# Unread products of ones at the norm boundaries, a later square, and feed-forward rounds over two weight tiles

## Chip, core and metric

The kernel runs on one core of one Trainium2 chip. The metric is the device time of one launch in microseconds (us), the median of the runs. The engines of the core are TensorE (PE, matrix products; PEld is its loading of stationary tiles), VectorE (DVE), ScalarE (ACT), GpSimd (POOL) and SyncE (SP, which issues the DMA transfers here).

## What is computed

One layer of an encoder on 256 tokens of width 2048, in float32: a SwiGLU feed-forward block, attention with 16 heads, and a second feed-forward block, each behind an RMS norm that a modulation vector scales and shifts.

```python
mod = jax.nn.silu(c) @ w_ada + b_ada
sh1, sc1, gt1, sh2, sc2, gt2, sh3, sc3, gt3 = jnp.split(mod, 9, axis=-1)
f = swiglu(modulate(rms_norm(h, g_ffn1), sh1, sc1), w1_gate, w1_up, w1_down)
h = h + 0.5 * gt1 * f
qkv = modulate(rms_norm(h, g_mix), sh2, sc2) @ w_qkv
...
h = h + gt2 * (jnp.concatenate([o_na, o_dil], -1) @ w_o)
f = swiglu(modulate(rms_norm(h, g_ffn2), sh3, sc3), w2_gate, w2_up, w2_down)
h = h + 0.5 * gt3 * f
```

## The kernel before

**Layout.** Features lie on the 128 partitions, the 256 tokens on the free axis. `h` is 16 tiles of 128x256. A normed input `nx[k]` (16 tiles) is kept as two halves of 256 columns, a rounded part and the rest, so that a product in the fast float32 format loses little: the rounded weights (`hi`, the cast of L146 on ACT) are multiplied with both halves in one product of 512 columns (L353), the rest of the weights (`lo`, the subtraction of L149 on DVE) with the first half alone, in one of 256 columns (L355). In qkv (L637, L640) the weights are the moving side, and all products have 512 columns.

**The weight stream.** All weights pass through one stream of tiles of 128x1024, eight blocks of 128x128 each. A tile is loaded by SP (L140, five buffers), cast on ACT (L146) and subtracted on DVE (L149); of `hi` and `lo` there are four buffers each (`LOB`). `W.add` collects eight products, takes the next tile with `chunk`, and issues eight products with `hi`, then eight with `lo`: one *round*. `prepare` keeps the stream three tiles ahead (`AHEAD`) and, at a rate given by `pace`, interleaves the 144 products of the modulation vector (*ada*, L129, 2.3 us each on DVE, with 1 MB of weights each).

**Stages.** A startup with six input tiles as the first rounds allow (L514); the first feed-forward's up products (`pa`, `pb`), its down products (`pd`, L417 adds them to `h`) over 32 of the 44 hidden tiles, then up and down over the other 12; qkv as 96 units of one tile with the attention heads woven in; the output projection as 32 units (`wo_unit`, `pso`); the second feed-forward in the same way as the first. The ends of the first feed-forward and of the output projection are the two *norm boundaries* of this text: `Stat` squares each tile of `h` (ACT, L195; the last one on DVE, L193) and adds the squares up on DVE (L185); TensorE sums them over the partitions by a product with ones (L208, L209); `rstd_from` turns that into the norm's factor (L168 to L173); `norm_pair` makes two `nx` tiles (L222 on DVE, L223 on ACT, L225 on DVE). TensorE's next product needs the first pair. The other seven pairs follow while the first eight units or rounds run; unit or round number *i* needs pair *i* (counted from 0).

**What sets the order.** Outside of `manual_schedule` a scheduler orders each engine's instructions at build time; in the range of the boundaries (`BORDER`: PE, DVE, ACT) they stand as the program writes them. Every engine works through its instructions in order.

## Time and profile before

| | |
|---|---|
| time, median of 3 runs | 1939.87 us (1939.45 to 1940.7) |
| time of the profiled execution | 1940.85 us |
| its span, first to last instruction | 1939.0 us |
| PE busy | 1900.1 us (98%) |
| DVE busy | 1524.3 us (79%) |
| ACT busy | 902.8 us (47%) |
| first product of L514 in the startup | 19.40 us |
| end of the first feed-forward, first qkv product | 768.6 us, 775.08 us |
| last product of the output projection, first of the second feed-forward | 1179.1 us, 1195.88 us |

A row of the trace's timeline gives the start and the length of a merged run of equal instructions; products overlap by their tails, so the pace of a run is read from start to start. PEclk is the TensorE clock that was granted, as a share of 2.4 GHz; 0.50 is 1.2 GHz.

### The profile page before, as it was taken

How to read it: one execution, taken by the hardware profiler on the slowest of the kernel's cores; microseconds unless marked ns; L12 is line 12 of the kernel's file. 1: busy time of each engine (PE TensorE's matmuls, PEld its weight loads, DVE VectorE, ACT ScalarE, POOL GpSimd, SP SyncE). 2: the span in 40 equal slices, each digit the busy share in tenths (PEclk: the TensorE clock that was granted, in tenths of full speed). 3: DMA queues.
4: the chain of work that ended last, by engine and by line, in shares of the span. 5: the costliest groups of instructions: out<-in, count | busy, mean ns of one | idle time of the engine just before them, and what ended most of it. 6: DMA issues, size and time to landing. Idle time of an engine off the chain costs nothing.

```text
span 1939.0 us, 27422 instructions
## 1 busy us (share of the span) xinstructions
PE 1900.1 (98%) x10528; PEld 1653.7 (85%) x10528; DVE 1524.3 (79%) x2058; ACT 902.8 (47%) x1327; POOL 0.7 (0%) x6
## 2 busy tenths in 40 slices
PE   8999999999999998999999997999999999999999
PEld 6888888888888887888788886888888888888888
DVE  7999999999788888799977897668865655545665
ACT  2545444433344454555555654544444433334442
POOL 0000000000000000000000000000000000000000
PEclk9999999999999999999999998999999999999999
DMA  9998888889988888589854453669866556656664
GB/s 400 404 362 310 312 309 302 312 330 408 343 308 341 314 312 292 199 329 323 321 192 163 153 157 105 198 213 321 321 206 186 189 189 187 193 187 188 190 194 134
DMA packets 120084, 503.98 MB, mean 260 GB/s; under 512 B 13329, under 2 KB 15633, under 8 KB 101521
## 3 DMA queue, kind: packets, MB, share of 16 engines
q1 hardware_dynamic: 119952, 502.24, 73.8%
q8 instruction: 82, 1.34, 0.3%
q14 instruction: 50, 0.40, 0.1%
HBM read 500.09 MB, written 2.10 MB: 259 GB/s over the span
## 4 chain that ended last, share of the span: by engine, by line
PE 90%; DVE 5%; DMA 2%; issue 1%; ACT 1%; SPq 0%; ACTq 0%; DVEq 0%
PE pb L353 29%; PE pd L353 16%; PE pb L355 15%; PE pd L355 8%; PE pqv L637 3%; PE pqk L637 3%; PE pqq L637 3%; PE pa L353 3%; PE pa L514 2%; DVE low L149 2%; PE pqv L640 2%; DMA ra<-in_w_ada_dram 2%; PE pa L355 1%; PE pqk L640 1%; PE pqq L640 1%
## 5 line engine op out<-in xcount | busy, mean ns | idle before, releaser
L146 ACT CAST hiw<-rw 128x1024 fp32r<-128x1024 f32 x644 | 674.0, 1050 | 784.5 <-PE pd L353 228.8
L149 DVE TENSOR_TENSOR low<-rw,hiw 128x1024 fp32r<-128x1024 f32 x644 | 782.7, 1221 | 302.7 <-ACT hiw L146 300.0
L353 PE MATMUL pb<-nx,hiw 128*128 128x512 f32 x2432 | 610.7, 393 | 4.1 <-DVE nx L225 4.1
L353 PEld LDWEIGHTS pb<-nx,hiw 128*128 128x128 f32 x2432 | 438.5, 189 | 83.3 <-issue 4.8
L355 PEld LDWEIGHTS pb<-nx,low 128*128 128x128 f32 x2432 | 332.3, 191 | 24.8 <-DVE low L149 1.2
L353 PE MATMUL pd<-hd,hiw 128*128 128x512 f32 x1384 | 346.7, 392 | 0.0
L355 PE MATMUL pb<-nx,low 128*128 128x256 f32 x2432 | 339.9, 283 | 0.5 <-DVE low L149 0.5
L353 PEld LDWEIGHTS pd<-hd,hiw 128*128 128x128 f32 x1384 | 248.9, 189 | 44.4
L129 DVE CUSTOM_DVE_ANT_0 ra<-ra,cb,vec 128x2048 f32<-128x2048 f32 x109 | 255.6, 2345 | 15.7 <-DMA ra<-in_w_ada_dram 15.3
L355 PEld LDWEIGHTS pd<-hd,low 128*128 128x128 f32 x1408 | 191.8, 190 | 14.0 <-DVE low L149 0.7
L355 PE MATMUL pd<-hd,low 128*128 128x256 f32 x1408 | 196.4, 282 | 0.3 <-DVE low L149 0.3
L417 DVE SCALAR_TENSOR_TENSOR h<-pd,m,h 128x256 f32<-128x256 f32 x126 | 59.4, 480 | 57.6 <-PE pd L355 57.2
L129 DVE CUSTOM_DVE_ANT_0 rx<-rx,cb,vec 128x2048 f32<-128x2048 f32 x35 | 82.1, 2345 | 3.7 <-DMA rx<-in_w_ada_dram 3.7
L353 PE MATMUL pa<-nx,hiw 128*128 128x512 f32 x288 | 72.3, 393 | 0.0
L637 PE MATMUL pqv<-hiw,nx 128*128 128x512 f32 x256 | 66.1, 401 | 3.5 <-ACT nx L223 3.5
L637 PE MATMUL pqk<-hiw,nx 128*128 128x512 f32 x256 | 65.0, 396 | 0.0
L637 PE MATMUL pqq<-hiw,nx 128*128 128x512 f32 x256 | 64.6, 394 | 0.0
L674 PE MATMUL pso<-ox,hiw 128*128 128x512 f32 x240 | 61.8, 401 | 0.0
L637 PEld LDWEIGHTS pqv<-hiw,nx 128*128 128x128 f32 x256 | 48.9, 194 | 13.9 <-ACT nx L223 3.9
L353 PEld LDWEIGHTS pa<-nx,hiw 128*128 128x128 f32 x288 | 51.9, 189 | 9.3
L637 PEld LDWEIGHTS pqq<-hiw,nx 128*128 128x128 f32 x256 | 46.8, 188 | 9.1
L637 PEld LDWEIGHTS pqk<-hiw,nx 128*128 128x128 f32 x256 | 46.5, 188 | 8.9
(145 smaller groups left out, 1380.9 us busy)
## 6 DMA issues: line engine op xcount, KB each, us to landing
ra<-in_w_ada_dram SPq DMA_DIRECT2D x109, 1024.0 KB, 7.3
rw<-in_w_b_dram SPq DMA_DIRECT2D x200, 512.0 KB, 4.4
rw<-in_w_d_dram SPq DMA_DIRECT2D x128, 512.0 KB, 4.3
rw<-in_w_c_dram SPq DMA_DIRECT2D x96, 512.0 KB, 3.6
rw<-in_w_qkv_dram SPq DMA_DIRECT2D x96, 512.0 KB, 4.7
rx<-in_w_ada_dram SPq DMA_DIRECT2D x35, 1024.0 KB, 7.5
rw<-in_w_e_dram SPq DMA_DIRECT2D x48, 512.0 KB, 4.1
rw<-in_w_a_dram SPq DMA_DIRECT2D x44, 512.0 KB, 6.8
```

What stands on the lines that cost most here:

```text
L129: dot = nc.vector.tensor_tensor_reduce(out=raw, in0=raw, in1=cb, scale=1.0, scalar=vec[:, BA + i : BA + i + 1], op0=ALU.mult, op1=ALU.add, ...
L146: cast = nc.scalar.copy(hi, raw)
L149: nc.vector.tensor_tensor(lo, raw, hi.bitcast(F32), ALU.subtract)
L353: nc.tensor.matmul(out, w, r, start=first, stop=False)
L355: nc.tensor.matmul(out[:, :S], lo[:, b * P : (b + 1) * P], r[:, 0, :], start=False, stop=last)
L417: nc.vector.scalar_tensor_tensor(h[d], part_, gate(d), h[d], ALU.mult, ALU.add)
L514: nc.tensor.matmul(pa[f][:, q, :], w[:, b * P : (b + 1) * P], full[k], start=k == 0 and q == 0, stop=k == K1 - 1 and q == 1, skip_group_ch ...
L637: nc.tensor.matmul(ps[t], nx[k][:, i, t * P : (t + 1) * P], whi[:, kk * 512 : (kk + 1) * 512], start=k + i == 0, stop=False)
L640: nc.tensor.matmul(ps[t], nx[k][:, 0, t * P : (t + 1) * P], wlo[:, kk * 512 : (kk + 1) * 512], start=False, stop=k == KT - 1)
L674: nc.tensor.matmul(ps, w, o, start=kk == 0, stop=False)
```

## The change

`keep_warm(n)` multiplies `ones` with `ones` n times into a bank that nobody reads. It is called with 16 in the startup ahead of L514, and at both norm boundaries with 4 ahead of the two products of the statistic and with 13 behind them.

In the last six units of the output projection the square of a tile of `h` is taken within the next unit, behind that unit's copy on ACT. At both boundaries one weight tile fewer is prepared ahead of the statistic (`ws.ahead`), and it follows behind the first pairs.

`W.add` takes two tiles at a time (`group`) from the first feed-forward's `ffn_rest` on, and in the second feed-forward from its third hidden tile on; the last four output tiles of each feed-forward go by single tiles as before. In the second feed-forward every other group is *turned*: its `lo` products come first if the group before it ended in `lo`, apart from accumulators that are new in it. The host lays out the weights of the up products accordingly (`halves`).

```diff
@@ -46,6 +46,8 @@
 AHEAD = 3
 RAWB = 5
 WARM = 8
+WA = 4
+WB = 13
 ARA = 2
 ARX = 1
 LOB = 4
...
@@ -86,6 +88,12 @@
+
+        def keep_warm(n):
+            ps = bank("warm")
+            for i in range(n):
+                nc.tensor.matmul(ps[:, :P], ones, ones, start=True, stop=True)
...
@@ -305,6 +313,10 @@
                 self.ready = {}
                 self.rate = 0.0
                 self.credit = 0.0
+                self.ahead = AHEAD
+                self.group = 1
+                self.turn = False
+                self.ended_lo = False

             def fetch(self, n):
                 while self.head < n:
@@ -315,7 +327,8 @@
                 self.tail += 1
                 return self.ready.pop(self.tail - 1)

-            def prepare(self, ahead=AHEAD, pin=False):
+            def prepare(self, ahead=None, pin=False):
+                ahead = self.ahead if ahead is None else ahead
                 while self.head <= min(self.tail + ahead, len(srcs) - 1):
                     self.ready[self.head] = wsplit(wraw(srcs[self.head]), pin)
                     self.head += 1
...
-            def chunk(self):
-                self.prepare()
+            def chunk(self, ahead=None):
+                self.prepare(ahead)
                 self.tail += 1
                 return self.ready.pop(self.tail - 1)

-            def add(self, out, r, first, last, then=None, whole=False):
-                self.todo.append((out, r, first, last, whole))
+            def add(self, out, r, first, last, then=None, whole=False, key=None):
+                self.todo.append((out, r, first, last, whole, key))
                 if then:
                     self.thens.append(then)
-                if len(self.todo) < 8:
+                if len(self.todo) < 8 * self.group:
                     return
-                hi, lo = self.chunk()
+                tiles = [self.chunk(self.ahead - i) for i in range(self.group)]
                 todo, thens = self.todo, self.thens
                 self.todo, self.thens = [], []
-                for b, (out, r, first, last, whole) in enumerate(todo):
-                    w = hi[:, b * P : (b + 1) * P]
+                new = {t[5] for t in todo if t[2]}
+                early = [b for b, t in enumerate(todo) if t[5] not in new] if self.turn and self.ended_lo else []
+                late = [b for b in range(len(todo)) if b not in early]
+
+                def weights(b, half):
+                    return tiles[b // 8][half][:, b % 8 * P : (b % 8 + 1) * P]
+
+                def low(b, stop):
+                    out, r = todo[b][:2]
+                    nc.tensor.matmul(out[:, :S], weights(b, 1), r[:, 0, :], start=False, stop=stop)
+
+                for b in early:
+                    low(b, False)
+                for b, (out, r, first, last, whole, key) in enumerate(todo):
+                    w = weights(b, 0)
+                    stop = last and b in early
                     if whole:
                         nc.tensor.matmul(out[:, :S], w, r[:, 0, :], start=first, stop=False)
-                        nc.tensor.matmul(out[:, :S], w, r[:, 1, :], start=False, stop=False)
+                        nc.tensor.matmul(out[:, :S], w, r[:, 1, :], start=False, stop=stop)
                     else:
-                        nc.tensor.matmul(out, w, r, start=first, stop=False)
-                for b, (out, r, first, last, whole) in enumerate(todo):
-                    nc.tensor.matmul(out[:, :S], lo[:, b * P : (b + 1) * P], r[:, 0, :], start=False, stop=last)
+                        nc.tensor.matmul(out, w, r, start=first, stop=stop)
+                for b in late:
+                    low(b, todo[b][3])
+                self.ended_lo = bool(late)
                 for then in thens:
                     then()

@@ -376,10 +406,13 @@
             tc.keep_in_program_order(nc.scalar.copy(part[f], ps))

         def up_mm(ps, k0, k1, first, last, then=None):
-            for j in range(2):
-                for k in range(k0, k1):
-                    end = k == k1 - 1
-                    ws.add(ps[:, j, :], nx[k], first and k == k0, last and end, then if end and j else None)
+            step = 8 if k1 - k0 == KT else k1 - k0
+            for ka in range(k0, k1, step):
+                for j in range(2):
+                    for k in range(ka, ka + step):
+                        end = k == k1 - 1
+                        ws.add(ps[:, j, :], nx[k], first and k == k0, last and end, then if end and j else None,
+                               key=(id(ps), j))

         def up_finish(f, ps, part, hid):
             if f in part:
@@ -404,8 +437,12 @@
                     acc_[d] = bank("pd")
                 if stat is not None and d == KT // 2 and f == fs[0]:
                     bg_until(0)
-                if order is not None and d == KT - 4 and f == fs[0]:
-                    order.enter_context(tc.manual_schedule(engines=BORDER))
+                if fs[-1] == FT - 1 and d == KT - 4 and f == fs[0]:
+                    ws.group, ws.turn = 1, False
+                    if order is not None:
+                        order.enter_context(tc.manual_schedule(engines=BORDER))
+                if stat is not None and d == KT - 1 and f == fs[4]:
+                    ws.ahead = AHEAD - 1
                 whole = d == KT - 1 and fs[-1] == FT - 1
                 end = f == fs[-1]

@@ -416,11 +453,15 @@
                     for part_ in (ps[:, :S], ps[:, S:])[: 1 if whole else 2]:
                         nc.vector.scalar_tensor_tensor(h[d], part_, gate(d), h[d], ALU.mult, ALU.add)
                     if stat is not None:
+                        if d == KT - 1:
+                            keep_warm(WA)
                         stat.add(h[d], late=d >= KT - 4)
+                        if d == KT - 1:
+                            keep_warm(WB)
                     if out is not None:
                         nc.sync.dma_start(out[d], h[d])

-                ws.add(acc_[d], hid[f], f == fs[0], end, update if end else None, whole)
+                ws.add(acc_[d], hid[f], f == fs[0], end, update if end else None, whole, key=d)

         def ffn(kx, part, ready_k, gate, stat=None, out=None, order=None):

...
         def ffn_rest(hid, gate, stat=None, out=None, order=None):
+            ws.group = 2
             psum_pool("bank")
             up_rate = ws.rate
...
         with tc.manual_schedule(engines=STARTUP):
-            warm = bank("warm")
-            for i in range(WARM):
-                nc.tensor.matmul(warm[:, :P], ones, ones, start=True, stop=True)
+            keep_warm(WARM)
...
+        with tc.manual_schedule(engines=STARTUP):
+            keep_warm(2 * WARM)
...
+            sqs = []
...
@@ -660,11 +703,22 @@
                     gt2 = mods[5]
                     if u < END - 1:
                         nc.scalar.copy(t, ps[:, :S])
+                    while sqs:
+                        hst.add(h[sqs.pop()], late=True)
+                    if u < END - 1:
                         nc.vector.tensor_tensor(t, t, ps[:, S:], ALU.add)
+                    if u == END:
+                        hst.fold()
                     nc.vector.scalar_tensor_tensor(t, t if u < END - 1 else ps[:, :S], gt2[:, d : d + 1], rows[b], ALU.mult, ALU.mult)
                     nc.vector.tensor_tensor(h[d], h[d], t, ALU.add)
-                    if b == 1:
-                        hst.add(h[d], late=u > END - TAIL)
+                    if u == END:
+                        keep_warm(WA)
+                        hst.add(h[d])
+                        keep_warm(WB)
+                    elif u >= END - TAIL:
+                        sqs.append(d)
+                    elif b == 1:
+                        hst.add(h[d])

                 def go(whi, wlo):
                     ps = bank("pso")
@@ -782,6 +836,7 @@
...
                     if u == END - 2 * TAIL:
                         bg_until(0)
+                    ws.ahead = AHEAD - (u in (0, END))
                     units[u](*ws.chunk())
                     for c in pairs_after.get(u, ()):
                         norm_pair((2 * c, 2 * c + 1), r2, 3, 4)
@@ -818,12 +873,14 @@
         for k in range(KT):
             for f in range(NG):
                 for j in range(2):
-                    ws.add(ps2[f][:, j, :], nx[k], k == 0, k == KT - 1)
+                    ws.add(ps2[f][:, j, :], nx[k], k == 0, k == KT - 1, key=(f, j))
...
+            ws.ahead = AHEAD if k else AHEAD - 1
         order.close()
         for f in range(NG):
             up_finish(f, ps2[f], {}, hid)
+        ws.group, ws.turn = 2, True
         ws.pace(RF)
         for f in range(NG, F1):
             ps = pair("pb")
...
+        def halves(x):
+            return x.reshape(-1, 2, 2, 8, P, P).transpose(0, 2, 1, 3, 4, 5)
+
...
             arr["w2_a"] = stream(gu[:NG].transpose(2, 0, 1, 3, 4))
-            arr["w2_b"] = stream(gu[NG:F1])
-        arr[f"w{l}_c"] = stream(gu[F1:])
+            arr["w2_b"] = stream(halves(gu[NG:F1]))
+        arr[f"w{l}_c"] = stream(halves(gu[F1:]))
```

PE in the second feed-forward's up products, twelve rows from the middle; `nx_99` to `nx_114` are the 16 input tiles. Before:

```order
L355 MATMUL pb<-nx_112,low 128x256
L355 MATMUL pb<-nx_113,low 128x256
L355 MATMUL pb<-nx_114,low 128x256
L353 MATMUL pb<-nx_99,hiw 128x512
L353 MATMUL pb<-nx_100,hiw 128x512
L353 MATMUL pb<-nx_101,hiw 128x512
L353 MATMUL pb<-nx_102,hiw 128x512
L353 MATMUL pb<-nx_103,hiw 128x512
L353 MATMUL pb<-nx_104,hiw 128x512
L353 MATMUL pb<-nx_105,hiw 128x512
L353 MATMUL pb<-nx_106,hiw 128x512
L355 MATMUL pb<-nx_99,low 128x256
```

and in the changed kernel, where two tiles were taken and the second group is turned:

```order
L371 MATMUL pb<-nx_109,low 128x256
L371 MATMUL pb<-nx_110,low 128x256
L371 MATMUL pb<-nx_111,low 128x256
L371 MATMUL pb<-nx_112,low 128x256
L371 MATMUL pb<-nx_113,low 128x256
L371 MATMUL pb<-nx_114,low 128x256
L382 MATMUL pb<-nx_107,hiw 128x512
L382 MATMUL pb<-nx_108,hiw 128x512
L382 MATMUL pb<-nx_109,hiw 128x512
L382 MATMUL pb<-nx_110,hiw 128x512
L382 MATMUL pb<-nx_111,hiw 128x512
L382 MATMUL pb<-nx_112,hiw 128x512
```

Before, eight `hi` products stand between eight `lo` products and the next eight. After, the rows are from the middle of a turned group: the `lo` products of two groups (32) adjoin, and the `hi` products behind them adjoin those of the next group (32).

ACT near the end of the output projection: `wt` takes an output tile from PSUM, `sq` is a square of a tile of `h` (`h2` holds tiles 8 to 11, `h3` 12 to 15). Before:

```order
L146 CAST hiw_10990<-rw_10988 128x1024
L662 COPY wt_11012<-pso_10994 128x256
L195 ACTIVATE sq_11017<-h3_93 128x256
L146 CAST hiw_11021<-rw_11019 128x1024
L662 COPY wt_11043<-pso_11025 128x256
L195 ACTIVATE sq_11048<-h3_93 128x256
```

and in the changed kernel:

```order
L154 CAST hiw_11026<-rw_11024 128x1024
L705 COPY wt_11048<-pso_11030 128x256
L203 ACTIVATE sq_11050<-h2_92 128x256
L154 CAST hiw_11057<-rw_11055 128x1024
L705 COPY wt_11079<-pso_11061 128x256
L203 ACTIVATE sq_11081<-h3_93 128x256
```

Before, the square behind a copy is that of the same tile (the copy of tile 12, the square of `h3`); after, it is that of the tile before (the copy of tile 12, the square of `h2`).

DVE in the first qkv units, between the pair of `nx6`, `nx7` and the next pair; `low` is the `lo` part of a weight tile. Before:

```order
L225 SCALAR_TENSOR_TENSOR nx6_105<-nt_7148,m3_81,nx6_105 128x256
L225 SCALAR_TENSOR_TENSOR nx7_106<-nt_7151,m3_81,nx7_106 128x256
L149 TENSOR_TENSOR low_7159<-rw_7156,hiw_7158 128x1024
L222 SCALAR_TENSOR_TENSOR nt_7174<-h2_92,m4_82,rsr_7071 128x256
L222 SCALAR_TENSOR_TENSOR nt_7177<-h2_92,m4_82,rsr_7071 128x256
```

and in the changed kernel:

```order
L233 SCALAR_TENSOR_TENSOR nx6_105<-nt_7181,m3_81,nx6_105 128x256
L233 SCALAR_TENSOR_TENSOR nx7_106<-nt_7184,m3_81,nx7_106 128x256
L157 TENSOR_TENSOR low_7192<-rw_7189,hiw_7191 128x1024
L157 TENSOR_TENSOR low_7198<-rw_7195,hiw_7197 128x1024
L230 SCALAR_TENSOR_TENSOR nt_7213<-h2_92,m4_82,rsr_7104 128x256
L230 SCALAR_TENSOR_TENSOR nt_7216<-h2_92,m4_82,rsr_7104 128x256
```

One subtraction stood between the pairs, now there are two: the tile that was prepared ahead of the statistic before. The same holds in the second feed-forward's first rounds.

## Rows read from the trace of the kernel before

**Rows 1.** PE's longest wait of all: line, waited for, total us, times, longest.

```profile
PE pstat L208 <- DVE sqa L185: 11.7, 2, 10.2
```

**Rows 2.** Stretches: length, PE, PEld, DVE, ACT, POOL busy, PEclk, DMA share, GB/s.

```profile
16.28:23.10 6.82, 3.70 (x9) 2.99 (x10) 6.32 (x12) 0.91 (x2) 0.00 (x0) 0.50 1.01 423
774.04:780.86 6.82, 5.78 (x14) 4.58 (x15) 6.09 (x15) 3.49 (x8) 0.00 (x0) 0.50 0.57 220
1183.64:1200.70 17.06, 7.23 (x18) 5.08 (x19) 13.92 (x28) 6.39 (x14) 0.00 (x0) 0.50 0.30 93
1320.00:1360.00 40.00, 40.00 (x233) 35.26 (x232) 36.26 (x42) 19.68 (x27) 0.00 (x0) 1.00 0.93 325
```

**Rows 3.** PE's timeline (start, length), second feed-forward: first and last of 33 round starts.

```profile
1402.07 2.00 PE L353 MATMUL pb<-nx,hiw 128*128 128x512 f32 x8
...
1491.46 2.00 PE L353 MATMUL pb<-nx,hiw 128*128 128x512 f32 x8
```

**Rows 4.** PE's timeline, qkv: starts of two units, four units apart.

```profile
786.07 1.98 PE L637 MATMUL pqv<-hiw,nx 128*128 128x512 f32 x8
...
796.95 1.98 PE L637 MATMUL pqv<-hiw,nx 128*128 128x512 f32 x8
```

**Rows 5.** PE's timeline, first feed-forward's end: sixteen products of 256 columns, then eight.

```profile
765.56 0.28 PE L350 MATMUL pd<-hd,hiw 128*128 128x256 f32 x1
...
767.48 1.12 PE L355 MATMUL pd<-hd,low 128*128 128x256 f32 x8
```

**Rows 6.** Timeline of all engines, first norm boundary.

```profile
769.88 0.48 DVE L417 SCALAR_TENSOR_TENSOR h<-pd,m,h 128x256 f32<-128x256 f32 x1
...
770.87 0.70 PE L209 MATMUL pstat<-sq,ones 128*128 128x256 f32 x2
...
775.08 3.78 PE L637 MATMUL pqv<-hiw,nx 128*128 128x512 f32 x8 [3.51 <-ACT nx L223]
...
793.73 0.87 DVE L222 SCALAR_TENSOR_TENSOR nt<-h,m,rsr 128x256 f32<-128x256 f32 x2
```

**Rows 7.** DVE's timeline, output projection: one period of a steady unit.

```profile
1154.48 1.22 DVE L149 TENSOR_TENSOR low<-rw,hiw 128x1024 fp32r<-128x1024 f32 x1
...
1157.26 1.22 DVE L149 TENSOR_TENSOR low<-rw,hiw 128x1024 fp32r<-128x1024 f32 x1
```

**Rows 8.** Timeline of all engines, second norm boundary.

```profile
1173.65 0.42 ACT L195 ACTIVATE sq<-h 128x256 f32<-128x256 f32 x1 [2.73 <-DVE h L665]
...
1178.00 0.42 ACT L195 ACTIVATE sq<-h 128x256 f32<-128x256 f32 x1 [2.73 <-DVE h L665]
1178.01 1.10 PE L679 MATMUL pso<-ox,low 128*128 128x256 f32 x8
1178.32 1.03 ACT L146 CAST hiw<-rw 128x1024 fp32r<-128x1024 f32 x1
...
1189.10 0.48 DVE L664 SCALAR_TENSOR_TENSOR wt<-pso,m,rsr 128x256 f32<-128x256 f32 x1
...
1190.54 1.22 PE L209 MATMUL pstat<-sq,ones 128*128 128x256 f32 x2
...
1195.88 3.75 PE L353 MATMUL pb<-nx,hiw 128*128 128x512 f32 x8 [4.12 <-DVE nx L225]
...
1210.38 0.87 DVE L222 SCALAR_TENSOR_TENSOR nt<-h,m,rsr 128x256 f32<-128x256 f32 x2
...
1213.92 0.88 DVE L222 SCALAR_TENSOR_TENSOR nt<-h,m,rsr 128x256 f32<-128x256 f32 x2
1214.98 0.88 DVE L225 SCALAR_TENSOR_TENSOR nx<-nt,m,nx 128x256 fp32r<-128x256 f32 x2 [0.18 <-ACT nx L223]
...
1217.71 2.00 PE L353 MATMUL pb<-nx,hiw 128*128 128x512 f32 x8
```

**Rows 9.** Timeline of the startup: eight products of 256 float32 columns; PEld's wait.

```profile
8.76 3.66 PE L484 MATMUL pstat<-sq,ones 128*128 128x256 f32 x16
...
55.81 6.77 PEld L514 LDWEIGHTS pa<-xf,rw 128*128 128x128 f32 x32 [0.20 <-ACT xf L235]
```

## The prediction

> **What bounds the kernel now.** The page gives PE as busy for nearly the whole span, so I read first where it is not. In the list of PE's waits one line stands out: the product of the norm statistic waits for DVE's sum of squares, once for 10.2 us [rows 1]. The timeline there shows why: the last product of the output projection ends at 1178.01 + 1.10 = 1179.11, DVE adds it only at 1189.10, the statistic starts at 1190.54, and the next feed-forward at 1195.88 [rows 8]. The first boundary has the same shape but is short: last product 767.48 + 1.12 = 768.60 [rows 5], DVE's addition 769.88, statistic 770.87, next product 775.08 [rows 6]. Then I read the granted clock by stretches: it falls to 0.50 (1.2 GHz) in the startup and at both boundaries, after PE sat idle, and in each of these PE works a while at that level [rows 2]. Last I read the pace of the products where PE never waits, which is most of the time: 32 rounds from 1402.07 to 1491.46 are 89.39 us, 2.793 us a round of eight products of 512 and eight of 256 columns [rows 3].
>
> **The rounds.** What should a round take? In qkv all products have 512 columns: four units of twelve from 786.07 to 796.95 are 10.88 / 48 = 0.2267 us each [rows 4]. Sixteen products of 256 columns from 765.56 to 767.48 take 0.120 each [rows 5]. Eight and eight at these paces are 1.813 + 0.960 = 2.773 us. The round takes 2.793, so the change from one kind to the other and back costs about 0.020. Grouping two tiles halves the number of such pairs, turning halves it again. By the order of the two programs the first feed-forward goes from 130 pairs to 65 in the stretches that are grouped, the second from 250 to 68: 65 + 182 = 247 pairs fewer, 247 x 0.020 = 4.9 us (1.3 and 3.6). All of it is on the path, since PE waits for nothing there. Bounds: nothing, if the loss hangs on something else; 6.7 if the longer runs shed 0.027 a pair, all that the start of a 512-column run seems to lose (an estimate: 0.020 plus the 0.007 that a first 256-column product gains). I take 4.9.
>
> The Trainium skill (TensorE: Matmul & The Clock Gate, Back-to-back issue gap) gives the gap of an isolated product by its columns alone, N / 2.4 + 2.5 ns, with no term for a change of size. The rows disagree in both paces (226.7 for its 215.8 ns at 512, 120 for 109 at 256), so I take the rows. By that rule this term would be nothing; that is a rival below.
>
> What the grouping could cost: a turned group ends in `hi`, so its `hi` buffers come free only at its end, and the next turned group, one group of 5.55 us later, begins with `lo`. Its second tile is needed 5.55 + 0.96 = 6.5 us after the buffer is free, and cast (1.03 [rows 8]) and subtraction (1.22 [rows 7]) take 2.3: some 4.2 us are left for what is queued ahead on ACT and DVE. I cost it at nothing; DVE is busy for 36.26 of 40 us at its fullest there [rows 2], with single operations of up to 2.3 us, so a few waits of tenths are possible (0 to 2 us).
>
> **The second boundary.** In the last units the period before is 1178.00 - 1173.65 = 4.35 us from square to square [rows 8], against PE's 2.8: ACT's square waits for DVE's last addition of the same tile, the next cast stands behind the square, and DVE's subtraction and additions wait for that cast. So DVE falls behind PE by about 1.5 us a unit. With the square one tile later it waits for nothing, and the period is DVE's own work: subtraction, square's sum, add, scale, add, which in a steady unit take 1157.26 - 1154.48 = 2.78 us back to back [rows 7]. That is PE's pace. The last scale then starts when the last product is there, 1179.11, or with half a microsecond of arrears at 1179.6 (two sums of squares now stand just ahead of it). I take 1179.6: 9.5 us earlier. The four unread products end long before the statistic's second product (four of 128 columns are half of the 3.66 / 8 = 0.46 us that 256 columns take [rows 9], 0.9 together), so they delay nothing.
>
> Clock: the statistic's second product takes 1.22 at half clock and 0.70 at full clock [rows 6, 8]. With 4 and 13 unread products (17 x 0.23 = 3.9 us) PE is idle for about 1.5 us at a time, and I expect full clock: 0.5 more. The first round would start 10.0 earlier, at 1185.9.
>
> The rest of that clock gain is mostly not PE's to take. Round 0 alone no longer loses 2.3 us, so round 7 would be due at 1185.9 + 7 x 2.793 = 1205.4. It needs pair 7. The pairs come from DVE, one each 1213.92 - 1210.38 = 3.54 us with a subtraction between [rows 8], and there is now one subtraction more ahead of pair 4. Pair 7's first DVE step was at 1213.92, and would be at 1213.92 - 10.0 + 1.14 = 1205.0; `nx` is there 1.5 later (first L225: 1214.98 + 0.45) [rows 8]. So round 7 starts near 1206.6, 1.2 after it is due: PE waits about 0.4 us at each of rounds 5, 6 and 7. Against 1217.71 the boundary gives **11.1 us**. Bounds: 12.3 if the pairs come in time; 6 if the arrears shrink by half only.
>
> **The first boundary.** One subtraction leaves the way, so DVE adds at 768.64 instead of 769.88. Four unread products (768.4 to 769.35) and the statistic's first product (0.45) then set its second at 769.8, 1.07 earlier than 770.87; without them it would be 1.2. The first qkv product comes at 774.0 instead of 775.08, with 13 unread products over by 773.2. At full clock unit 7 would be due at 774.0 + 7 x 2.72 = 793.04. Here too the extra subtraction (1.14) eats the lead of 1.07: pair 7's first step stays at 793.8 [rows 6], `nx` follows 1.0 later (in qkv the first products need ACT's half alone), so unit 7 starts at 794.8 instead of 796.95: **2.1 us**. Bounds: 3.9 if the pairs are in time; 1.0 if the clock falls all the same. DVE has idle time right behind (units 8 to 15), so it can follow.
>
> **The startup.** Sixteen unread products (3.6 us) fill half of the idle time ahead of L514. But even if all of the 3.70 us of work at half clock [rows 2] ran at full clock, 1.85 us, it would not last: at 55.81 the weight load of the last input tile waits for `xf` [rows 9], which hangs on ada products and their loads. **0**; not below nothing either, as they follow the statistic, which ends at 8.76 + 3.66 = 12.42, and are over at 16.1, 3.3 us ahead of L514's first product.
>
> **Sum.** 4.9 + 11.1 + 2.1 + 0 = 18.1 us off the profiled span of 1939.0: 1920.9. What lies around the span is 1.85 in that execution (1940.85), but 0.87 against the median of the runs, 1939.87; on the median the forecast is 1939.87 - 18.1 = **1921.8**.
>
> **Rivals.** *The rounds give nothing* (the loss belongs to each tile and not to the change of size): 1939.87 - 13.2 = 1926.7. Against it speaks that qkv's rounds of 512 columns alone show 0.2267 without loss [rows 4]. 0.10. The rule of the Trainium skill weighed above (TensorE: Matmul & The Clock Gate, Back-to-back issue gap) would give this time. *The pairs are not the limit at the boundaries* (the subtraction is hidden, full clock counts): 1.2 and 1.8 more, 1918.8. Against it: DVE's 3.5 us a pair against 2.8 a round. 0.12. *The last units stay tied* through another wait of ACT (copy for PE, cast for copy), half of the arrears remain: 5 less at the second boundary, 1926.8. 0.07. *Slower: turned groups wait for weights.* The second feed-forward has 62 turned groups; if each waited over 18.1 / 62 = 0.29 us at its first `lo` products, all is lost, and at 0.5 us the time is 1953. It decides once ACT's and DVE's queues delay a tile by over 4.2 us; DVE is that full in one stretch of 40 us, where four or five groups lie, not in 62 groups. 0.04.
>
> **Chances.** The forecast holds 0.67, its own range 1919.5 to 1924.5. The range reaches to both neighbours with the bounds of the rounds: **1917.5 to 1927.5**. A measurement can tell about 0.2% (3.9 us) here: faster than 1936.0 has 0.93, within 0.2% 0.03, slower 0.04.
>
> **What would show it.** Right: rounds of two tiles at 5.57 us, four of a turned pair at 11.11; the last scale of the output projection within 1 us of PE's last product; 1.00 in the granted clock at both boundaries; PE waits of about 0.4 us for DVE's `nx` ahead of rounds 5 to 7 and units 5 to 7; the last `xf` still waited for near 55.8. Wrong: PE waiting for `low` or `hiw` in the second feed-forward (the slower rival); starts of 512-column runs that lose the same per tile; a period over 3 us in the last units; a clock of 0.50 behind either boundary.

## The result: 1922.8 us, and the profile after

The changed kernel takes 1922.77 us, median of six runs (1921.25 to 1924.95), against 1940.41 of the kernel before beside it (1939.45 to 1941.75): a ratio of 0.9911, 95% interval 0.9898 to 0.9923, 17.6 us less. The forecast was 1921.8, with 1917.5 to 1927.5 as its range. The profiled execution took 1921.25, with a span of 1919.5.

Where the time went is read by places that both programs have. PE's stage starts in the two profiled executions, all in us:

| stretch on PE | before | changed | less by |
|---|---|---|---|
| start to the first statistic | 8.76 | 8.57 | 0.19 |
| from there to the first `pb` product | 154.79 | 154.69 | 0.10 |
| to the end of the first feed-forward | 605.05 | 604.18 | 0.87 |
| first boundary: to the 13th unit of qkv | 41.96 | 39.83 | 2.13 |
| attention: to the first product of the output projection | 262.84 | 261.59 | 1.25 |
| output projection, to the end of its last product | 105.72 | 104.14 | 1.58 |
| second boundary: to the ninth round | 41.39 | 29.93 | 11.46 |
| from there to PE's end | 715.38 | 713.38 | 2.00 |

That is 19.6 in these two executions. The page's busy times hardly differ, since PE's products are the same; what is gone is idle time and half clock. PE's list of waits (line, waited for, total, times, longest) no longer has the 10.2 us of [rows 1]:

```profile
PE pa L556 <- ACT xf L243: 3.2, 2, 3.0
...
PE pb L382 <- DVE nx L233: 1.9, 3, 1.2
PE pqv L680 <- ACT nx L231: 1.5, 3, 0.6
PE pb L371 <- DVE low L157: 1.4, 3, 0.6
...
PE pstat L217 <- DVE sq L201: 0.2, 1, 0.2
```

The second boundary in the timeline, to be held against [rows 8]. ACT's square stands 2.6 us behind the one before it, not 4.35; DVE's last scale (L712) starts at 1173.06, when PE's last product ends (1171.90 + 1.10 = 1173.00), where it was 10.0 late; the pairs (`nt`) then come 3.54 apart, with 4.67 once where two subtractions stand together.

```profile
1167.65 0.42 ACT L203 ACTIVATE sq<-h 128x256 f32<-128x256 f32 x1
...
1170.22 0.42 ACT L203 ACTIVATE sq<-h 128x256 f32<-128x256 f32 x1 [1.21 <-DVE h L713]
...
1171.90 1.10 PE L733 MATMUL pso<-ox,low 128*128 128x256 f32 x8
...
1173.06 0.48 DVE L712 SCALAR_TENSOR_TENSOR wt<-pso,m,rsr 128x256 f32<-128x256 f32 x1
...
1174.51 0.70 PE L217 MATMUL pstat<-sq,ones 128*128 128x256 f32 x2 [0.19 <-DVE sq L201]
1175.05 3.06 PE L96 MATMUL warm<-ones 128*128 128x128 f32 x26
...
1179.27 2.08 PE L382 MATMUL pb<-nx,hiw 128*128 128x512 f32 x8 [1.16 <-DVE nx L233]
...
1183.16 0.88 DVE L230 SCALAR_TENSOR_TENSOR nt<-h,m,rsr 128x256 f32<-128x256 f32 x2
...
1187.83 0.88 DVE L230 SCALAR_TENSOR_TENSOR nt<-h,m,rsr 128x256 f32<-128x256 f32 x2
...
1198.43 0.87 DVE L230 SCALAR_TENSOR_TENSOR nt<-h,m,rsr 128x256 f32<-128x256 f32 x2
...
1200.03 2.11 PE L382 MATMUL pb<-nx,hiw 128*128 128x512 f32 x8 [0.48 <-DVE nx L233]
```

The clock by stretches (length, the engines' busy time, PEclk, DMA share, GB/s), to be held against [rows 2]: of these stretches only the startup's is still at 0.50.

```profile
19.30:22.72 3.42, 3.42 (x10) 2.67 (x9) 3.38 (x5) 0.00 (x0) 0.00 (x0) 0.50 1.02 418
769.00:776.00 7.00, 6.45 (x42) 5.66 (x42) 6.33 (x15) 2.90 (x7) 0.00 (x0) 1.00 0.75 259
1174.00:1181.00 7.00, 5.65 (x38) 4.81 (x37) 6.32 (x14) 2.71 (x6) 0.00 (x0) 1.00 0.25 80
```

And PE's rounds, against [rows 3]: 32 products of `hi`, 32 of `lo`, four tiles in 1441.60 - 1430.49 = 11.11 us, where four rounds took 11.17.

```profile
1430.49 4.00 PE L371 MATMUL pb<-nx,low 128*128 128x256 f32 x32
1434.32 7.44 PE L382 MATMUL pb<-nx,hiw 128*128 128x512 f32 x32
1441.60 4.00 PE L371 MATMUL pb<-nx,low 128*128 128x256 f32 x32
```

### The profile page after: what moved, and what is told of

It is laid out like the page before. It is cut to its first block, busy times and chain, and to the rows that moved or that the text cites. A ratio compares the mean times of both kernels' runs of the same rounds, so it can differ in the third digit from the quotient of the medians.

```text
span 1919.5 us, 27613 instructions
## 1 busy us (share of the span) xinstructions
PE 1900.3 (99%) x10628; PEld 1660.5 (87%) x10628; DVE 1524.4 (79%) x2058; ACT 903.9 (47%) x1327; POOL 0.7 (0%) x6
## 4 chain that ended last, share of the span: by engine, by line
PE 85%; DVE 8%; DMA 3%; ACT 2%; issue 1%; SPq 0%; DVEq 0%; ACTq 0%
PE pb L382 27%; PE pd L382 16%; PE pb L371 14%; PE pd L371 9%; PE pqq L680 3%; DVE low L157 3%; PE pa L382 3%; PE pqk L680 3%; PE pqv L680 2%; DMA ra<-in_w_ada_dram 2%; PE pa L371 1%; PE pqq L683 1%; PE pqk L683 1%; PE pqv L683 1%; DVE ra L137 1%
## 5 line engine op out<-in xcount | busy, mean ns | idle before, releaser
L382 PE MATMUL pb<-nx,hiw 128*128 128x512 f32 x2432 | 581.1, 391 | 1.9 <-DVE nx L233 1.9
L382 PEld LDWEIGHTS pb<-nx,hiw 128*128 128x128 f32 x2432 | 446.8, 188 | 88.7 <-issue 1.3
L382 PE MATMUL pd<-hd,hiw 128*128 128x512 f32 x1384 | 328.4, 390 | 0.0
L371 PEld LDWEIGHTS pb<-nx,low 128*128 128x128 f32 x2432 | 312.1, 191 | 14.5 <-DVE low L157 2.7
L371 PE MATMUL pb<-nx,low 128*128 128x256 f32 x2432 | 316.7, 283 | 1.4 <-DVE low L157 1.4
L382 PEld LDWEIGHTS pd<-hd,hiw 128*128 128x128 f32 x1384 | 255.0, 188 | 49.7
L371 PEld LDWEIGHTS pd<-hd,low 128*128 128x128 f32 x1408 | 179.1, 191 | 6.8 <-DVE low L157 1.0
L371 PE MATMUL pd<-hd,low 128*128 128x256 f32 x1408 | 181.6, 283 | 0.4 <-DVE low L157 0.3
L423 ACT COPY gu<-pb 128x512 f32<-128x512 f32 x56 | 32.9, 587 | 52.7 <-PE pb L382 29.8
```

Source lines behind the costliest of these rows:

```text
L371: nc.tensor.matmul(out[:, :S], weights(b, 1), r[:, 0, :], start=False, stop=stop)
L382: nc.tensor.matmul(out, w, r, start=first, stop=stop)
L423: nc.scalar.copy(t, ps[:, :, :S])
```

## Experiments

Executions of one kernel differ by 2 to 8 us, so the effects below are read from the stretches of the table above, in one profiled execution of each kernel, and the times are given beside them. Comments in the code below are added here.

### The square alone (on the kernel before)

```diff
                     if u < END - 1:
                         nc.scalar.copy(t, ps[:, :S])
+                    while sqs:
+                        hst.add(h[sqs.pop()], late=True)
...
+                    if u == END:
+                        hst.fold()
...
-                    if b == 1:
-                        hst.add(h[d], late=u > END - TAIL)
+                    if u == END:
+                        hst.add(h[d])
+                    elif u >= END - TAIL:
+                        sqs.append(d)
+                    elif b == 1:
+                        hst.add(h[d])
```

> The kernel before with the later square alone: no unread products, rounds of one tile, no tile held back. Theory (ACT's square behind DVE's addition of the same tile makes DVE late by 1.5 us a unit): the period of the last units falls from 4.35 to 2.8 us, the last scale of the output projection starts within 1 us of PE's last product there, and the time falls by 9.5 us (ratio to the kernel before 0.9951). The clock behind the boundary stays at 0.50, which costs the first products of the feed-forward 2.3 us as before. Rival 1 (the cast or the copy keeps the units tied): a period of 3.4 us or more and a gain of 5 us or less. Rival 2 (the square gives more than I forecast, and the 15.6 us by which the changed kernel's second statistic came earlier are mostly its): a gain of over 10.5 us.

Measured: ratio 0.9948 (0.9931 to 0.9965), 9.6 us less. From PE's last product to the ninth round 32.06 us instead of 41.39: 9.33 less. ACT's and DVE's timeline in the last units: casts 2.74 apart, and the last scale (L670) 1.3 us behind PE's last product (1183.19 + 1.07 = 1184.26), because a subtraction of 1.22 still stands ahead of it.

```profile
1176.71 1.04 ACT L146 CAST hiw<-rw 128x1024 fp32r<-128x1024 f32 x1
...
1179.45 1.04 ACT L146 CAST hiw<-rw 128x1024 fp32r<-128x1024 f32 x1
...
1183.19 1.07 PE L689 MATMUL pso<-ox,low 128*128 128x256 f32 x8
...
1183.59 1.22 DVE L149 TENSOR_TENSOR low<-rw,hiw 128x1024 fp32r<-128x1024 f32 x1
...
1185.58 0.48 DVE L670 SCALAR_TENSOR_TENSOR wt<-pso,m,rsr 128x256 f32<-128x256 f32 x1
```

The theory holds for the period and the time, but not for the last scale, which was expected within 1 us. The square is over half of the whole change.

### The rounds alone, and rounds cut in half

Rounds alone, on the kernel before, with nothing else of the change:

```diff
-                hi, lo = self.chunk()
+                tiles = [self.chunk(self.ahead - i) for i in range(self.group)]
...
+        ws.group, ws.turn = 2, True                  # second feed-forward; first: group only
...
-            arr["w2_b"] = stream(gu[NG:F1])
+            arr["w2_b"] = stream(halves(gu[NG:F1]))
```

Rounds in halves, on the kernel before:

```diff
-                for b, (...) in enumerate(todo):            # eight with hi
-                for b, (...) in enumerate(todo):            # eight with lo
+                cuts = (0, 4, 8) if self.tail > w2_start + 8 else (0, 8)
+                for b0, b1 in zip(cuts, cuts[1:]):
+                    for b, (...) in list(enumerate(todo))[b0:b1]:   # four with hi
+                    for b, (...) in list(enumerate(todo))[b0:b1]:   # four with lo
```

> The kernel before with the rounds over two weight tiles (turned in the second feed-forward) alone. Theory (each change from 512 to 256 columns and back loses 0.020 us): rounds of two tiles at 5.57 us, turned pairs of them at 11.11, and 0.7 to 1.3 us less in the first feed-forward, 3.0 to 3.6 in the second, so 3.7 to 4.9 us less in all (ratio 0.9975 to 0.9981); nothing before 160 us, nothing between 700 and 1190 us. Rival 1 (the loss belongs to the tile): within 0.5 us of the kernel before, four tiles at 11.17 us. Rival 2 (turned groups wait for weights when nothing else has moved): waits of PE for low or hiw of over 2 us in sum, and a gain under 3 us.

> The kernel before with each round of the second feed-forward (from its ninth tile, 256 rounds) in two halves: four products of 512 columns, four of 256, four of 512, four of 256. The same products, one more pair of changes in each round. Theory (a pair of changes costs 0.020 us): a round goes from 2.793 to 2.813 us, 256 x 0.020 = 5.1 us slower (ratio 1.0026), and nothing before 1200 us. Rival (the loss belongs to the tile or to the reading of a new buffer): 2.793 us a round, no change. Second rival (short runs let PE's weight loads fall behind, since a 256-column product hides less of a load): over 2.84 us a round, more than 12 us slower.

Measured: rounds alone 0.9986 (0.9977 to 0.9996), 3.1 us less, where 3.7 to 4.9 were expected; halves 1.0020 (1.0011 to 1.0029), 2.9 us more. From the ninth round to PE's end the kernel before takes 715.38 in its profile and 715.38 again in that of the square alone; with rounds over two tiles, turned, 711.74, a gain of 3.64. So 182 pairs of changes fewer are 0.020 each. In the first feed-forward the gain is lost in this execution (604.9 us, where kernels without grouping take 604.5 to 605.1): PE waits 1.1 us for `low` there (0.3 in the changed kernel).

With halves the same stretch takes 718.76, 3.4 more: 0.013 for each of 256 additional pairs, not 0.020 as expected. The timeline shows half a round in 1.40:

```profile
1424.59 1.09 PE L357 MATMUL pb<-nx,hiw 128*128 128x512 f32 x4
1425.52 0.63 PE L359 MATMUL pb<-nx,low 128*128 128x256 f32 x4
1425.99 1.09 PE L357 MATMUL pb<-nx,hiw 128*128 128x512 f32 x4
```

Start to start, the products of a long run of 512 columns in the changed kernel take 233, 236, 228, 232, 231, and then 226.7 ns each; those of 256 columns 113, 119, and then 120. So a run of 512 loses about 27 ns in its first five products and one of 256 gains 8: 20 ns a pair. A run of four ends before all of that is lost: half a round takes 1.403, where four and four at the full pace are 1.387, so each pair there costs 0.017. Two of them cost 0.033 a round, 0.013 more than the one of 0.020 before, and that is what was measured. The loss hangs on the change of size: in the halves no tile is added, and in qkv, where `hi` and `lo` alternate as well but all products have 512 columns, nothing is lost [rows 4].

The rule of the Trainium skill that the prediction weighed (TensorE: Matmul & The Clock Gate, Back-to-back issue gap) has the gap of an isolated product hang on its columns alone, by which both kernels would have been at the time of the kernel before; both traces speak against it, with 3.64 less and 3.4 more.

### Two tiles, but not turned

```diff
-        ws.group, ws.turn = 2, True
+        ws.group, ws.turn = 2, False
```

> The changed kernel with the second feed-forward's rounds over two tiles but not turned. From the ninth tile of the second feed-forward to PE's end the kernel before takes 715.4 us, the kernel before with rounds over two tiles and turned 711.7 (no waits in it), the changed kernel 713.4 with 0.9 of waits for low. Theory (each pair of changes costs 0.020, 117 pairs of the 182 go by grouping alone): 713.0 without waits, 1.3 more than turned. Since a group that isn't turned begins with hi, its first wait would be for hiw, and what low needs has 3.6 us more: waits for low under 0.2. Rival (turning gives the whole gain, grouping none): 715. Rival on the waits (grouping, not turning, makes DVE late): waits for low of 0.5 us or more here too.

Measured: 0.9914 (0.9900 to 0.9929); from the ninth round to the end 712.88, with no wait for `low` in it. Forecast 713.0. Grouping gives 2.5, turning another 1.1 where nothing waits (711.74 in four traces). In the changed kernel (713.4) waits for `low` of 0.62 and 0.25, and slower products behind them, eat that. Ahead of the longer one DVE had waited 1.94 us for an ada row, and its dot of 2.35 stood ahead of the subtractions (the changed kernel's timeline):

```profile
1306.10 2.35 DVE L137 CUSTOM_DVE_ANT_0 ra<-ra,cb,vec 128x2048 f32<-128x2048 f32 x1 [1.94 <-DMA ra<-in_w_ada_dram]
...
1308.98 1.22 DVE L157 TENSOR_TENSOR low<-rw,hiw 128x1024 fp32r<-128x1024 f32 x1
...
1310.25 0.98 PE L371 MATMUL pb<-nx,low 128*128 128x256 f32 x6 [0.62 <-DVE low L157]
```

### The first feed-forward turned too

```diff
         def ffn_rest(hid, gate, stat=None, out=None, order=None):
-            ws.group = 2
+            ws.group, ws.turn = 2, True
```

> The changed kernel with the first feed-forward's groups turned too. Theory (45 pairs of changes fewer, 0.020 each): 0.9 us less between 163 and 766 us. Rival (DVE, which has the ada dots of 2.3 us there, doesn't get low ready for a group that begins with it): the waits for low near 425 to 434 us (0.3 in the changed kernel, 1.3 in the kernel with rounds alone) grow past 1.5 us and there is no gain, or a loss of up to 2 us.

Measured: 0.9929 (0.9915 to 0.9944), 1926.1 us; the first feed-forward takes 607.2 instead of 604.2. The rival happened, with 3.0 lost where up to 2 were expected, and at 414 us, not near 425 to 434. DVE's and PE's timeline where PE waited longest:

```profile
407.36 2.34 DVE L137 CUSTOM_DVE_ANT_0 rx<-rx,cb,vec 128x2048 f32<-128x2048 f32 x1
...
408.80 3.32 PE L371 MATMUL pd<-hd,low 128*128 128x256 f32 x24
409.63 1.21 DVE L157 TENSOR_TENSOR low<-rw,hiw 128x1024 fp32r<-128x1024 f32 x1
...
410.83 2.34 DVE L137 CUSTOM_DVE_ANT_0 ra<-ra,cb,vec 128x2048 f32<-128x2048 f32 x1
...
413.10 1.22 DVE L157 TENSOR_TENSOR low<-rw,hiw 128x1024 fp32r<-128x1024 f32 x1
...
414.38 1.22 PE L371 MATMUL pd<-hd,low 128*128 128x256 f32 x8 [2.27 <-DVE low L157]
```

Between two subtractions stands one dot each; a group that begins with `lo` needs the tile 3.6 us sooner than one that begins with `hi`, and DVE, busy for 19.05 of the 20 us from 400, doesn't give it. This is the slower rival of the prediction, and in the first feed-forward DVE is that full from 200 us on; the changed kernel doesn't turn there.

### The tile held back: for no step, for one, for all

```diff
-                    ws.ahead = AHEAD - (u in (0, END))              # one step
+                    ws.ahead = AHEAD - (u < 8 or u == END)          # all
...
-            ws.ahead = AHEAD if k else AHEAD - 1
+            ws.ahead = AHEAD if k == KT - 1 else AHEAD - 1
```

and for none:

```diff
-                if stat is not None and d == KT - 1 and f == fs[4]:
-                    ws.ahead = AHEAD - 1                             # end of the first feed-forward
...
-                    ws.ahead = AHEAD - (u in (0, END))
...
-            ws.ahead = AHEAD if k else AHEAD - 1
```

> The changed kernel with no tile held back at the boundaries: three tiles prepared ahead always, so DVE's subtraction of a fourth tile stands ahead of the last addition again and none stands between the pairs in its place. I read from the end of PE's last product ahead of a boundary to the 13th qkv unit (changed kernel 39.8 us, before 42.0) and to the ninth round (29.9, before 41.4). Theory (the subtraction costs its 1.2 us once, ahead of the statistic or ahead of pair 4): first statistic product 1.2 later at the second boundary, the first qkv product and the first round 1.2 later, but no waits ahead of units 5 to 7 (1.1) and rounds 6 and 7 (0.7): 39.9 and 30.4. Rival (holding the tile back is worth its 1.2 at each boundary): 41.0 and 31.1. In all 0.5 or 2.4 us slower than the changed kernel.

> The changed kernel with the tile held back until all pairs are made (units 0 to 7, rounds 0 to 7), not only for the first unit and the first step: one subtraction between two pairs, never two. Theory (pairs 4 to 7 come 1.14 earlier, the waits of units 5 to 7, 1.1 in all, and of rounds 6 and 7, 0.7, go): from PE's last product to the 13th unit 38.7 instead of 39.8, to the ninth round 29.2 instead of 29.9, so 1.8 us less in all. Rival (the lead that is then one tile smaller is missing as soon as the tile is made up): a wait for low or hiw of 0.5 us or more at units 8 to 10 or rounds 8 to 10, and no gain.

Measured: none 0.9914 (0.9899 to 0.9928), all 0.9904 (0.9887 to 0.9920). By the boundaries, in us from PE's last product:

| | to the first product behind it | to the 13th unit | to the first round | to the ninth round |
|---|---|---|---|---|
| held for one step (changed) | 5.21 | 39.83 | 6.27 | 29.93 |
| for none | 6.47 | 39.93 | 7.30 | 29.84 |
| for all | 5.21 | 40.02 | 6.47 | 29.83 |

Nothing of it matters by the 13th unit or the ninth round. For none was as expected, but for the ninth round (29.84, not 30.4). For all, my theory failed: the pairs came earlier, and PE waited for weights in their place, at units 6 and 7 already and not at 8 to 10 (PE's waits there: line, waited for, total, times, longest).

```profile
PE pqv L680 <- ACT hiw L154: 1.0, 2, 0.5
PE pqv L680 <- ACT nx L231: 0.6, 1, 0.6
```

In all three kernels DVE makes the later pairs 3.54 us apart. So moving whole subtractions ahead of the pairs or behind them changes nothing here; what the order inside a pair does is the next run.

### The subtraction inside the pair

```diff
+            if defer[0]:                     # units 1 to 4; the rounds ahead of pairs 4 to 7
+                subs.append(sub)
...
         def norm_pair(ks, r, jsh, jsc):
             for k in ks:                     # nt on DVE, nx on ACT
...
+            while subs:
+                subs.pop(0)()
             for k, t in zip(ks, ts):         # second half of nx on DVE
```

> The changed kernel with DVE's subtraction of a weight tile put between the two halves of a pair, for pairs 4 to 7 at both boundaries: cast, the pair's two first steps, the subtraction, the pair's two last steps, where it was cast, subtraction, first steps, last steps. The same operations. Theory (holding a tile back, for one step, for all or not at all, gave the same time, since DVE's 3.54 us a pair set it; 0.45 of these are an idle wait for the cast, which stood behind nx on ACT, and 0.18 a wait for nx): 3.0 to 3.1 us a pair, the waits ahead of units 5 to 7 and rounds 6 and 7 go, 38.8 instead of 39.8 to the 13th unit, 29.3 instead of 29.9 to the ninth round: 1.7 us less in all. Rival (the cast waits for a buffer that PE frees, and with nx queued behind it on ACT the pairs come later still): 40 or more, and 30 or more.

Measured: 0.9895 (0.9881 to 0.9908), 1919.75 us, against 1923.14 for the changed kernel beside it: the fastest kernel of this study. 37.99 to the 13th unit and 28.69 to the ninth round, 1.84 and 1.24 less. DVE's timeline in the changed kernel, of one pair, and in this one:

```profile
788.05 1.23 DVE L157 TENSOR_TENSOR low<-rw,hiw 128x1024 fp32r<-128x1024 f32 x1 [0.46 <-ACT hiw L154]
...
789.20 0.87 DVE L230 SCALAR_TENSOR_TENSOR nt<-h,m,rsr 128x256 f32<-128x256 f32 x2
...
790.25 0.88 DVE L233 SCALAR_TENSOR_TENSOR nx<-nt,m,nx 128x256 fp32r<-128x256 f32 x2 [0.18 <-ACT nx L231]
...
791.59 1.23 DVE L157 TENSOR_TENSOR low<-rw,hiw 128x1024 fp32r<-128x1024 f32 x1 [0.45 <-ACT hiw L154]
```

```profile
782.78 0.87 DVE L237 SCALAR_TENSOR_TENSOR nt<-h,m,rsr 128x256 f32<-128x256 f32 x2
...
783.58 1.22 DVE L160 TENSOR_TENSOR low<-rw,hiw 128x1024 fp32r<-128x1024 f32 x1
...
784.71 0.87 DVE L242 SCALAR_TENSOR_TENSOR nx<-nt,m,nx 128x256 fp32r<-128x256 f32 x2
...
785.50 0.87 DVE L237 SCALAR_TENSOR_TENSOR nt<-h,m,rsr 128x256 f32<-128x256 f32 x2
```

In the first, idle 0.45 for the cast and 0.18 for `nx`: 3.54 a pair. In the second none: 2.72, PE's own pace in qkv. I had expected 3.0 to 3.1; the three steps follow one another closer than their lengths (0.87, 1.22 and 0.87 in 2.72). The gain is larger than the waits that were listed (1.1 and 0.7), since the products behind a wait are slower too (0.34, then 0.23 to 0.24 us, where the pace is 0.227): in the changed kernel units 5 and 6 take 3.53 each and unit 7 2.88, not 2.72.

### Without the unread products

The 4, 13 and 16 added products left out; run twice, the second time beside the changed kernel on one chip.

```diff
-                            keep_warm(WA)
-                            keep_warm(WB)
...
-            keep_warm(2 * WARM)
...
-                        keep_warm(WA)
-                        keep_warm(WB)
```

> The changed kernel without any of its added unread products (4 and 13 at both boundaries, 16 in the startup; the eight of the kernel before stay). Theory (the clock counts where the pairs don't cover it): the granted clock is 0.50 behind both boundaries. Behind the first the qkv products lose 3.4 us, of which the waits of units 5 to 7 (0.1 + 0.49 + 0.49) cover 1.1, and the start is up to 0.3 later or earlier: unit 7 some 2 us later against the changed kernel. Behind the second the rounds lose 2.4 us, the statistic 0.5, the waits of rounds 6 and 7 cover 0.7: 2.2 us. Startup 0.3. In all 4 to 5 us slower than the changed kernel, 1926.5 against 1922.5. Rival (the pairs of DVE set the time, as my forecast had it): unit 7 and round 7 within 0.7 us of those of the changed kernel, in all 1 to 1.5 us slower. Second rival (the clock stays at 1.00 without the unread products, since the later square shortens PE's idle time): no change, and 1.00 in the stretches behind the second boundary.

> The changed kernel without the added unread products, once more, now beside the changed kernel on one chip: before, the two stood on different chips, 1928.7 and 1922.8 us. Theory 1 (only the second boundary gains by them): 0.6 us slower than the run beside it, 30.5 instead of 29.9 to the ninth round, 39.8 to the 13th unit, and what was more came from the chip and the loads. Theory 2 (the clock is worth more than the boundaries show): 4 to 6 us slower, with half-clock stretches in the attention stage that the run beside it doesn't have. Theory 3 (only the startup counts besides): 2 to 3 us slower, with the 1.7 us of a longer half-clock stretch there lost for good.

> The changed kernel once more, unaltered, beside the next run on the same chip. All accounts: 17 to 18 us less than the kernel before (ratio 0.9909 to 0.9913); from PE's last product ahead of a boundary to the 13th qkv unit 39.8 us, to the ninth round 29.9. In the attention stage (13th qkv unit to the first product of the output projection) the traces so far show 259.5 to 267.4 us, in kernels that are alike there. If that spread comes from DVE's waits for the ada rows' loads, its waits for these loads there and PE's waits for pP and pT rise and fall together, PE's some 0.5 us below DVE's.

Measured: 0.9930 (0.9915 to 0.9945), and the second time 0.9946 (0.9932 to 0.9959), 1929.06 us, where the changed kernel beside it has 0.9917 (0.9904 to 0.9931), 1923.14: 16.9 less than the kernel before, where 17 to 18 were expected. The clock is at 0.50 behind both boundaries:

```profile
771.45:778.28 6.83, 4.92 (x12) 3.87 (x13) 6.22 (x16) 2.73 (x6) 0.00 (x0) 0.50 0.66 228
1184.46:1191.29 6.83, 4.56 (x13) 3.82 (x14) 6.22 (x16) 2.89 (x7) 0.00 (x0) 0.50 0.19 73
```

And yet the boundaries lose little: 39.77 and 40.24 to the 13th unit (with them 39.8), 30.50 and 30.78 to the ninth round (29.93 and 30.13). PE's first unit takes 4.45 and 5.12 us there, its first round 4.65 and 4.95 (with them 2.84 to 2.87), but behind these it waits for no pair: they are ready when it comes. With the unread products PE is there sooner and waits for the same pairs. Unit 7 and round 7 come 0 to 0.8 us later without them, as the first run's rival had it, not 2. So the pairs leave little of the clock's worth, as forecast. What the unread products are worth in the kernel of the last section, where PE waits for none but the first pair, was not run.

But the medians differ by 5.9 us, and their intervals don't overlap; the first run's 1928.74 is 6.0 above the changed kernel's 1922.77. In the two profiled executions of the second run PE's end differs by 4.5: start and first feed-forward 0.4, boundaries 1.1, attention stage 2.0, output projection 1.8, and 0.8 the other way in the second feed-forward. In the attention stage and the projection the kernel without unread products has two stretches at half clock that the other doesn't have; each follows a wait of PE.

```profile
901.16:904.57 3.41, 3.41 (x10) 2.64 (x9) 1.97 (x4) 2.03 (x5) 0.00 (x0) 0.50 0.94 357
1092.31:1095.72 3.41, 3.41 (x14) 3.02 (x13) 3.28 (x8) 1.10 (x2) 0.00 (x0) 0.50 0.58 167
```

One such stretch costs about 1.6 us: the output projection takes 103.9 to 104.2 in the executions without one, 105.5 to 105.8 with one, 107.1 to 107.3 with two. Over all fourteen traces, in the attention stage proper, five of the six executions without unread products have one, none of the eight with them. Each follows one wait of 2.15 to 2.57 us, or two close together of 2.19 and 2.25 in sum; in the eight executions the longest wait was 1.55 and the largest such sum 1.66. In the projection every execution has the same waits (2.0, and 1.25 with 1.32 close behind), and the clock falls behind them in about half of the executions of either kind.

So theory 1 gives what the boundaries show, but its 0.6 us in all is missed by 5. What theory 2 named was seen (4 to 6 us, half-clock stretches in the attention stage), but not shown to come from leaving the products out: four of the five executions with such a stretch ran on one chip, on which no kernel with unread products was profiled, and why PE's waits in the attention stage are longer without them, 130 us behind the last of them, is open. The stretches in the projection are no sign of it, since they come with either kind. Theory 3 (the startup alone) does not fit: 0.4 by the end of the first feed-forward.

### The loads of the ada rows

What makes PE wait in the attention stage at all? Here the dots of the attention stage read one row block that is loaded once:

```diff
         def ada_issue(i):
+            if fixed:
+                return fixed[0]
```

> The changed kernel with the ada rows of the attention stage left out: DVE's dots there all read one row block that is loaded once, so none waits for a load; all other instructions are the same. What it computes from there on is not the reference's. Theory (PE waits there because DVE, busy for 98% of the stretch, waited for the loads of ada rows): no waits of DVE for ada rows, waits of PE for pP and pT under 0.5 us, the stage at 259.5 to 260.5 us from the 13th unit to the output projection. Rival (DVE's work is too much there by itself): waits for pP and pT of 1.5 us or more, and 261.5 us or more. The loads left out also free the DMA queues for the weights, which could shorten the rest by tenths; the output projection's own stage, 104 to 107 us, tells that.

Measured: 0.9901 (0.9888 to 0.9915), 1920.41 us, 2.7 less than the changed kernel beside it, with intervals that overlap; the attention stage takes 260.2, where that has 264.3. DVE's waits for ada rows up to 976 us and PE's waits in the stage (line, waited for, total, times, longest); first the changed kernel beside it, then without the loads, where DVE has no row for `ra` any more:

```profile
DVE ra L137 <- DMA ra<-in_w_ada_dram: 4.7, 5, 1.5
...
PE pP L786 <- DVE sc L780: 2.9, 2, 1.6
PE pT L748 <- DVE qn L648: 1.5, 2, 0.8
```

```profile
PE pT L752 <- DVE qn L652: 0.6, 1, 0.6
PE pP L790 <- DVE sc L784: 0.2, 1, 0.2
```

The theory holds but for a rest of 0.8 us of waits (0.5 expected). Across the traces the two go together: DVE 1.4, PE 0; 2.1 and 1.8; 3.1 and 3.0; 3.6 and 2.9; 4.5 and 3.8; 5.1 and 4.8; 6.3 and 5.8, and the other kernels with loads in between. With 1.4 the stage took 259.5, no more than without the loads. How late the loads are differs from execution to execution (4.7 and 2.1 us in the two of the changed kernel), and the attention stage has the widest spread of the stretches that are alike in all kernels, 259.5 to 267.4 us, with the half-clock stretches that follow.

## The prediction, step by step

- **Second boundary, 11.1 forecast, 11.46 in the trace.** The tie of square and addition was read rightly: 9.33 by the square alone, 9.5 forecast. The remaining 2.1 come from the unread products or the held tile. From 32.06 with neither, the unread products alone lead to 29.84, the held tile alone to 30.50 and 30.78, and both together to no less (29.93). The prediction had half a microsecond for the clock and left the rest to DVE's pairs; that the two are cures for the same loss it did not see.
- **Pairs as the limit: right for the changed kernel.** Rounds 6 and 7 and units 6 and 7 wait for `nx`, 0.22 to 0.49 each, about 0.4 forecast; units there start 3.53 apart. Round 5 and unit 5 don't wait. The price of the rival (1.2 and 1.8 more) is what the subtraction inside the pair then took: 1.24 and 1.84.
- **First boundary, 2.1 forecast, 2.13.** Unit 7 starts at 793.51, 20.9 us behind the first qkv product, as worked out (20.8). Here too either of the two is enough: 39.93 to the 13th unit with the unread products alone, 39.77 and 40.24 with the held tile alone, 41.2 to 42.0 in the four kernels with neither.
- **Rounds, 4.9 forecast; 2.9 in the two profiled executions.** The price of 0.020 a pair of changes was right (3.64 for 182). The term that was mis-sized is the waits for `low`: costed at nothing, with 0 to 2 us as their bound. In the second feed-forward of the changed kernel the list has 0.9 of them (0 to 1.3 in other executions), and with the slower products behind them they take 1.64 of the 3.64. In the first 0.87 of 1.3 is left, and on the mean of ten traces with grouping 0.3 (604.4 against 604.7 in three without): near 432 us PE waits 0.2 to 1.1 for `low` with grouping, 0 to 0.3 without. Two things stand in DVE's way. In the second feed-forward it is an ada dot that had waited for its load right ahead (0.9 to 4.3 us, in four of the five traces with such waits). Near 432 us it is a dot of 2.35 and five additions to `h` of 2.05 together, ahead of one subtraction.
- **Startup, 0 forecast:** 0.1 from the first statistic to `pb`, the wait for `xf` at 55.52 as foretold.
- **Not foreseen:** 1.25 and 1.58 in the attention stage and the output projection, which the sum had at nothing. The first goes with DVE's waits for loads (3.1 and 2.1 us), the second with a half-clock stretch at 1132.44 that this execution of the kernel before has and that of the changed kernel hasn't. Neither is shown to be the change's doing. Nor did the prediction expect that leaving the unread products out would cost 5.9 us in the median, of which the boundaries show 1.1.

So the mechanisms at the boundaries were right, but that the sum came so near is in part luck. The two profiled executions differ by 19.6: the rounds give 2.0 less than forecast, and what was not foreseen 2.8 more. The medians differ by 17.6, 0.5 less than the forecast's 18.1.

The slower rival decided nothing in the second feed-forward, but it is real: turning the first cost 3.0 us there.

## To carry to other kernels

Where three engines hand a tile round, look for an operation that waits for the last step of the same tile while the next tile's first step stands behind it in the queue; taking it one tile later costs nothing and here gave 9 of 18 us. When moving work within an engine's queue changes nothing, look at that engine's idle time between operations: here three places for a subtraction gave the same time, and putting it between two dependent steps gave 3 us more. Before a reordering is costed at nothing, check the queue of the engine that feeds it for long operations and for those that wait for a load; the latter come late in some executions only.

## What the runs showed of the hardware

- A product of 512 columns loses time only in the first five of a run behind products of 256 columns, about 27 ns in all, and a run of 256 gains 8 in its first two: 20 ns a pair with 8 or more in a run, 17 with four.
- The granted clock fell to 0.50 behind the same PE waits (2.0 us; 1.25 and 1.32 close together) in about half of the executions of alike code, and each fall of 3.4 us cost 1.6. It fell behind the boundaries in all six executions without unread products there, and in none of the eight with them.
